# Block products for pair 2 of the first feed-forward part, and joined weight halves for the first dilated group's values

## The chip, the cores and the metric

One core of one Trainium2 chip runs the whole layer as one program. Its engines work side by side: TensorE (PE) multiplies, VectorE (DVE) and ScalarE (ACT) compute element by element, GpSimd (POOL) does a few small things, and SyncE (SP) issues nearly all transfers, one after another in program order. The metric is the device time of one execution in microseconds. The kernel before takes 1127.27 us (median of three runs, 1127.23 to 1127.75).

## What is computed

One decoder layer on 512 tokens of 1024 features in float32: a feed-forward half-step, a token mixer (sparse attention beside dilated attention, merged by gates), and a second feed-forward half-step. What matters here, cut from the reference:

```python
def swiglu(x, w_gate, w_up, w_down):
    return (jax.nn.silu(x @ w_gate) * (x @ w_up)) @ w_down
...
    h = rms_norm(x, ffn1_pre[l])
    x = x + 0.5 * rms_norm(swiglu(h, ffn1_w_gate[l], ffn1_w_up[l], ffn1_w_down[l]), ffn1_post[l])
    h = rms_norm(x, mix_pre[l])
    y = token_mixer(h, ...)
    x = x + rms_norm(y, mix_post[l])
    h = rms_norm(x, ffn2_pre[l])
    x = x + 0.5 * rms_norm(swiglu(h, ffn2_w_gate[l], ffn2_w_up[l], ffn2_w_down[l]), ffn2_post[l])
...
# dilated attention, for each of three (window, dilation) groups of four heads
    o, lse = banded_attention(strided(q), strided(k), strided(v), 1, window // dil, dil, slopes[gidx])
```

The feed-forward width is 2816, which is 22 blocks of 128.

## The kernel before

**Products in three parts.** To keep float32 precision every operand is split in a rounded high part and a low part: ScalarE casts the high part (`whi`, L112), VectorE subtracts it (`wlo`, L119). `mm3` (L141 to L143) then issues three matmuls: high by high, low by high, high by low. A `wsplit` of a 128x1024 piece is thus one ScalarE cast and one VectorE subtraction, and TensorE can't start a product before both parts stand.

**The feed-forward part** (`ffn`) goes through 11 pairs of feature blocks. A classical pair takes, for gate and up and both blocks, 8 steps of 128 input features with three matmuls of 512 tokens: 2 x 2 x 8 x 3 = 96 matmuls of 512 columns. The other pairs are done by `strassen(p)`: the pair's weights are four quarters (a11 and a12 are gate, a21 and a22 are up, each for one half of the 1024 input features), the tokens likewise, and Winograd's scheme makes gate and up with seven products in place of eight, on sums: 7 x 2 x 4 x 3 = 168 matmuls of 256 columns. The sums of the weights are made on VectorE, s1 = a21+a22 first, then a11-a21, s2 = s1-a11, and a12-s2. The sums of the tokens (`token_sums`, T1 to T4, in high and low parts) are made once, in steps taken from a list between the pairs. Before, pairs 3 to 10 of the first part are done in this way and pairs 0 to 2 classically.

**The down product** (`ffn_down`) is a scheme of seven products as well. It needs four sums of down weights for each pair (`down_sums`, T1 to T4, where T4 = b21 - T2). They are made ahead, while the pairs run (`weight_sums`, or `early_sums` from four separate blocks of 128x512), written to a tensor in memory (`tdram`), and loaded again when the products come. T4's product has 5 of its 11 weight blocks loaded into the tiles of the split tokens (`xl_t`, split there into `xh_t` and `xl_t`), which are free by then.

**Order.** Tiles come from pools, and a load waits until the last reader of its tile is done; the program's order on each engine is the order of the code. All loads and stores named here stand in one queue (SP): a transfer that waits holds all behind it. The gate and up weights of a Strassen pair are loaded at L361 in four pieces of 512 KB, the two quarters of the first half into one tile and those of the second half into another; of the second half the up quarter comes first.

**The dilated group 0's values** (from the line with `C_VD` on): for each of 4 groups of tokens, 8 steps of three matmuls of 256 columns; `keep` then stores a high part (ScalarE) and a low part (VectorE).

Of the kernel before, what the change touches and what calls it, by code (L numbers as in the profile page):

```python
# [63 lines left out]
class Layer:  # L64
# [237 lines left out]
    def ffn(self, n, wg, wu, wd, post, finish, xsrc, tags, nps, aside=None):  # L302
# [26 lines left out]
        def weight_sums(p):  # L329
# [6 lines left out]
            with self.tc.issue_after(self.last_rest):  # L336
                self.down_sums(*[r[:, e, h * S:(h + 1) * S] for e in range(2) for h in range(2)])
# [13 lines left out]
        def strassen(p):  # L351
# [45 lines left out]
            weight_sums(p)  # L397
# [81 lines left out]
        self.ffn_down(E, X, Y, wd, post, finish, xsrc)  # L479

    def down_sums(self, b11, b12, b21, b22):

        for out, x, y in ((b11, b12, b11), (b12, b22, b12), (b22, b22, b11), (b21, b21, b22)):
            self.nc.vector.tensor_sub(out, x, y)

    def early_sums(self, p, wd, places):
# [20 lines left out]
    def token_sums(self):  # L507
# [9 lines left out]
        self.tsum = [([], []) for _ in range(4)]
        steps = []
        for c in range(2):
            hi, lo = [[v.rearrange("p (k c) -> p k c", k=2) for v in g]  # L520
                      for g in (places[8 * c:8 * c + 4], places[8 * c + 4:8 * c + 8])]
            if kept:
                whole = [kept[h][i][c] for i, h in ((0, 0), (1, 1), (0, 1), (1, 0))]
            else:
                whole = [self.slot("x").rearrange("p (k c) -> p k c", k=2) for _ in range(4)]
            f1, f2, f3, f4 = whole
# [1095 lines left out]
```

## Time and profile before

| | us |
|---|---|
| runs | 1127.23, 1127.27, 1127.75 |
| profiled execution | 1127.8 |
| its span on the core | 1125.6 |
| TensorE busy | 1115.7 (99%) |
| VectorE busy | 911.2 (81%) |
| ScalarE busy | 646.8 (57%) |
| moved by DMA | 206 MB |

The span runs from the first to the last instruction in the trace; 2.2 us of the execution's own time lie around it. In the rows below, a group or timeline row names the line of the kernel, the engine, the operation, and out<-in by the program's tile names; `SPq` is the queue of SyncE, whose rows show when a transfer was issued, not when it landed. `pb_S`, `pb_T`, `pb_V` and `pb_F` are accumulators of TensorE. The profile's clock was 1.00 in all stretches shown.

### The profile page before, as it was taken

What the parts mean: (1) busy time and instruction counts of PE and PEld (TensorE: products, weight loads), DVE (VectorE), ACT (ScalarE), POOL (GpSimd) and SP (SyncE); (2) the same over time, 40 slices, a digit from 0 to 9 for tenths busy, and PEclk for the clock granted to TensorE, in tenths of its full rate; (3) what the DMA queues carried; (4) which work ended last, traced back from release to release, by engine and by line L of the source; (5) the groups of instructions that cost most, each with busy time, mean ns of one, the idle gap of its engine ahead of it and who ended that gap; (6) DMA issues with size and microseconds to landing.
All of it is one profiled execution on the core that took longest, in us unless ns stands there. A gap on an engine that the chain in (4) does not pass through costs nothing.

```text
span 1125.6 us, 18656 instructions
## 1 busy us (share of the span) xinstructions
PE 1115.7 (99%) x6998; PEld 1004.2 (89%) x6998; DVE 911.2 (81%) x1565; ACT 646.8 (57%) x1169; POOL 79.2 (7%) x112
## 2 busy tenths in 40 slices
PE   9999999999999999999999999999999999999997
PEld 8889999998889987778888998888999999998886
DVE  7889999879677889687666688976898888979674
ACT  5435555567564778677565634645555555558562
POOL 1000000000012033243000000001000000000000
PEclk9999999999999999999999999999999999999999
DMA  9986665578863652211477758683323434356862
GB/s 318 331 283 224 185 208 173 153 267 293 265 206 108 196 132 85 68 37 47 147 246 237 243 174 289 203 290 121 101 87 126 129 112 126 100 187 228 290 224 82
DMA packets 153086, 206.04 MB, mean 183 GB/s; under 512 B 19842, under 2 KB 98210, under 8 KB 152740
## 3 DMA queue, kind: packets, MB, share of 16 engines
q1 hardware_dynamic: 152992, 204.85, 56.2%
q8 instruction: 55, 0.90, 0.3%
q14 instruction: 35, 0.29, 0.1%
q10 hardware_dynamic: 4, 0.00, 0.0%
HBM read 165.45 MB, written 39.37 MB: 182 GB/s over the span
## 4 chain that ended last, share of the span: by engine, by line
PE 90%; DVE 5%; ACT 2%; issue 1%; POOL 1%; DMA 1%; POOLq 0%; DVEq 0%; ACTq 0%
PE pb_F L141 11%; PE pb_F L143 11%; PE pb_F L142 11%; PE pb_S L143 8%; PE pb_S L142 8%; PE pb_S L141 8%; PE pb_T L143 6%; PE pb_T L142 6%; PE pb_T L141 6%; PE pb_V L143 3%; PE pb_V L142 3%; PE pb_V L141 3%; PE pb_V L1060 2%; PE pb_T L1045 1%; DVE SP_s L785 1%
## 5 line engine op out<-in xcount | busy, mean ns | idle before, releaser
L112 ACT CAST whi<-raw 128x1024 fp32r<-128x1024 f32 (+1 forms) x213 | 217.7, 1023 | 245.6 <-issue 71.1
L119 DVE TENSOR_TENSOR wlo<-raw,whi 128x1024 fp32r<-128x1024 f32 (+1 forms) x213 | 252.9, 1190 | 91.8 <-ACT whi L112 89.9
L141 PE MATMUL pb_F<-xh_t,whi 128*128 128x512 f32 (+1 forms) x392 | 142.0, 362 | 0.2 <-DVE Q_s L1270 0.2
L142 PE MATMUL pb_F<-xl_t,whi 128*128 128x512 f32 (+1 forms) x392 | 141.1, 360 | 0.0
L143 PE MATMUL pb_F<-xh_t,wlo 128*128 128x512 f32 (+1 forms) x392 | 141.0, 360 | 0.0
L112 ACT CAST whi<-tmp_t 128x1024 fp32r<-128x1024 f32 x55 | 57.6, 1048 | 57.4 <-PE pb_S L142 22.4
L119 DVE TENSOR_TENSOR wlo<-tmp_t,whi 128x1024 fp32r<-128x1024 f32 x55 | 67.3, 1224 | 23.2 <-ACT whi L112 21.8
L141 PEld LDWEIGHTS pb_F<-xh_t,whi 128*128 128x128 f32 x392 | 74.2, 189 | 9.9 <-DVE Q_s L1270 0.4
L143 PEld LDWEIGHTS pb_F<-xh_t,wlo 128*128 128x128 f32 x392 | 74.2, 189 | 9.6
L142 PEld LDWEIGHTS pb_F<-xl_t,whi 128*128 128x128 f32 x392 | 74.3, 190 | 9.3
L141 PE MATMUL pb_S<-xh_t,whi 128*128 128x256 f32 (+1 forms) x232 | 68.4, 295 | 0.0
L143 PE MATMUL pb_S<-xh_t,wlo 128*128 128x256 f32 (+1 forms) x232 | 68.3, 294 | 0.0
L142 PE MATMUL pb_S<-xl_t,whi 128*128 128x256 f32 (+1 forms) x232 | 68.3, 294 | 0.0
L1036 POOL TENSOR_SCALAR SP_s<-SP_s,st_t 128x384 f32<-128x384 f32 (+2 forms) x48 | 47.8, 1010 | 103.8 <-DVE st_t L972 76.3
L163 POOL TENSOR_TENSOR rs_t<-rs_t,mhalf_t 128x1 f32<-128x1 f32 x24 | 17.1, 711 | 538.1 <-DVE rs_t L159 538.0
L142 PE MATMUL pb_T<-xl_t,whi 128*128 128x256 f32 (+1 forms) x184 | 53.9, 293 | 0.0
L143 PE MATMUL pb_T<-xh_t,wlo 128*128 128x256 f32 (+1 forms) x184 | 53.8, 293 | 0.0
L141 PE MATMUL pb_T<-xh_t,whi 128*128 128x256 f32 (+1 forms) x184 | 53.7, 293 | 0.0
L141 PEld LDWEIGHTS pb_S<-xh_t,whi 128*128 128x128 f32 x232 | 44.5, 192 | 1.0
L142 PEld LDWEIGHTS pb_S<-xl_t,whi 128*128 128x128 f32 x232 | 44.5, 192 | 1.0
L143 PEld LDWEIGHTS pb_S<-xh_t,wlo 128*128 128x128 f32 x232 | 44.5, 192 | 0.9
L785 DVE CUSTOM_DVE_ANT_0 SP_s<-pb_S,W_s 128x128 f32<-128x128 f32 (+2 forms) x92 | 37.9, 441 | 7.0 <-PE pb_S L780 4.8
(839 smaller groups left out, 3425.3 us busy)
## 6 DMA issues: line engine op xcount, KB each, us to landing
raw<-in_ffn_w_up_dram SPq DMA_DIRECT2D x38, 512.0 KB, 4.9
raw<-in_ffn_w_gate_dram SPq DMA_DIRECT2D x37, 512.0 KB, 5.0
raw<-in_w_in_dram SPq DMA_DIRECT2D x18, 1024.0 KB, 5.5
raw<-in_ffn_w_down_dram SPq DMA_DIRECT2D x14, 1024.0 KB, 5.8
raw<-tdram SPq DMA_DIRECT2D x14, 1024.0 KB, 6.5
NN_s<-in_ffn_w_down_dram SPq DMA_DIRECT2D x22, 512.0 KB, 5.0
tdram<-NN_s SPq DMA_DIRECT2D x22, 512.0 KB, 4.4
odram<-ring_s SPq DMA_DIRECT2D x36, 128.0 KB, 3.2
```

The source lines that it names most:

```text
L112: self.last_cast = self.nc.scalar.copy(dsthi, src).ins
L119: self.last_rest = self.nc.vector.tensor_sub(dstlo, src, dsthi.bitcast(F32)).ins
L141: mm(out, lhi, rhi, start=start, stop=False, skip_group_check=skip)
L142: mm(out, lhi, rlo, start=False, stop=False, skip_group_check=skip)
L143: mm(out, llo, rhi, start=False, stop=stop, skip_group_check=skip)
L163: nc.gpsimd.tensor_tensor(out=r, in0=v, in1=self.mhalf, op=OP.pow)
L785: nc.vector.tensor_tensor_reduce(p, s, w, -1.0, FLOOR, OP.add, OP.min, st_m)
L1036: nc.gpsimd.tensor_scalar(pp, pp, st[:, 1, t:t + 1], None, op0=OP.mult)
L1045: nc.tensor.transpose(b[:, o + (t - kk) * P:o + (t - kk + 1) * P], pt[pn][:, po + kk * P:po + (kk + 1) * P], self.ident)
L1060: self.nc.tensor.matmul(out[:, kk * P:S], v, pp, start=first and kk == 0 and pi == 0, stop=False, skip_group_check=True)
```

## The change

Five things are edited:

1. Pair 2 of the first part is done by `strassen` (`STRASSEN`).
2. For this, the token sums are made earlier. Two of the four transposed token groups are also copied unsplit while they are still in the accumulator (`whole=True` at the last two `norm_T`), so that four of the eight sums of high and low part (`join`) go; the list of steps (`STEPS`) now gives five steps at once, then three, then two.
3. T4 of five pairs (`DEFER`: 0, 1, 2, 9, 10) is not made ahead: `down_sums` leaves out its fourth subtraction, and the fourth place in memory holds b21 itself. At the end of the first part `ffn_down` loads T2 and b21 of these five pairs into `xl_t` and `xh_t` (four loads in place of one) and subtracts there. Those five are T4's first blocks in place of pairs 0 to 4.
4. A Strassen pair makes the down sums of the pair before it, not its own, and the tiles that `early_sums` uses for pairs 4 to 7 are others (`SUM_TAGS`).
5. The values of dilated group 0: the high and the low part of the weights stand side by side, so that the high part of the tokens meets both in one matmul of 512 columns, and the low part of the tokens meets the high part in one of 256. The right half of the accumulator is added to the low part of the values by one more VectorE instruction for each token group.

```diff
-STRASSEN = range(3, NF // 2), range(1, NF // 2)
+STRASSEN = range(2, NF // 2), range(1, NF // 2)
+DEFER = 0, 1, 2, 9, 10
-STEPS = (0, 3, 3, 3, 3), (4, 2)
+STEPS = (5, 3, 2), (4, 2)
...
-                self.down_sums(*[r[:, e, h * S:(h + 1) * S] for e in range(2) for h in range(2)])
+                self.down_sums(*[r[:, e, h * S:(h + 1) * S] for e in range(2) for h in range(2)], p not in DEFER)
...
-            weight_sums(p)
+            if p - 1 in STRASSEN[n]:
+                weight_sums(p - 1)
...
-        for out, x, y in ((b11, b12, b11), (b12, b22, b12), (b22, b22, b11), (b21, b21, b22)):
+        for out, x, y in ((b11, b12, b11), (b12, b22, b12), (b22, b22, b11), (b21, b21, b22))[:3 + last]:
             self.nc.vector.tensor_sub(out, x, y)
...
-        nc.sync.dma_start(xl[:, 0:EARLY].bitcast(F32), weights["T4"](0, EARLY))
+        if defer:
+            for k, o, m in ((0, 0, 3), (3, NP - 2, 2)):
+                for v, nm in ((xl, "T2"), (xh, "T4")):
+                    nc.sync.dma_start(v[:, k:k + m].bitcast(F32), weights[nm](o, m))
+        else:
+            nc.sync.dma_start(xl[:, 0:EARLY].bitcast(F32), weights["T4"](0, EARLY))
         product(half(parts["O"], 0), "B21", a, False, True, lambda k: split_next("Y"))
         for k in range(0, EARLY, 2):
             ks = slice(k, min(k + 2, EARLY))
-            self.split(xh[:, ks], xl[:, ks], xl[:, ks].bitcast(F32))
+            src = xl[:, ks].bitcast(F32)
+            if defer:
+                d4 = self.sbt("tmp", [P, 2, S], bufs=2)[:, 0:ks.stop - k]
+                with self.tc.issue_after(self.last_rest):
+                    nc.vector.tensor_sub(d4, xh[:, ks].bitcast(F32), src)
+                src = d4
+            self.split(xh[:, ks], xl[:, ks], src)
...
-        ws = [self.wsplit(r[:, 4 * u:4 * u + 4], [4, 256]) for u in range(2)]
+        ws = []
+        for u in range(2):
+            for i, w in enumerate(self.wpair([2, 512])):
+                k = 4 * u + 2 * i
+                v = w.rearrange("p k (x f) -> p k x f", x=2)
+                self.split(v[:, :, 0], v[:, :, 1], r[:, k:k + 2])
+                ws.extend((w[:, j], v[:, j, 0]) for j in range(2))
...
-            for k in range(KT):
-                w = ws[k // 4]
-                self.mm3(b[:, 0:256], self.xh[k][:, c], self.xl[k][:, c], w[0][:, k % 4], w[1][:, k % 4], k == 0, k == KT - 1)
-            vt[0].append(keep(b[:, 0:256], 0, t))
+            for k, (both, hi) in enumerate(ws):
+                nc.tensor.matmul(b, self.xh[k][:, c], both, start=k == 0, stop=False, skip_group_check=True)
+                nc.tensor.matmul(b[:, 0:256], self.xl[k][:, c], hi, start=False, stop=k == KT - 1, skip_group_check=True)
+            v = keep(b[:, 0:256], 0, t)
+            nc.vector.tensor_add(v[:, :, 1], b[:, 256:512].rearrange("p (n d) -> p n d", n=4), v[:, :, 1].bitcast(F32))
+            vt[0].append(v)
...
-            t2 = self.norm_T(2, g, OPEN[2], sq2)
+            t2 = self.norm_T(2, g, OPEN[2], sq2, whole=True)
```

How this moves instructions is seen at three places. The first is SyncE's queue ahead of the first Strassen pair's weights. Before (pair 3; `raw_874` is its first half of gate and up, `raw_877` the second half, `KB_s` are the blocks of down weights of `early_sums`, `tdram` the memory of the sums; in brackets what a row waits for):

```order
L494 DMA tdram_72<-KB_s_681 128x512 [waits DMAHW7_49,DVE_49]
L490 DMA KB_s_779<-in_ffn1_w_down_dram 128x512 [waits DMAHW4_49,DMAHW0_49]
L490 DMA KB_s_780<-in_ffn1_w_down_dram 128x512 [waits DMAHW5_49,DMAHW1_49]
L490 DMA KB_s_781<-in_ffn1_w_down_dram 128x512 [waits DMAHW6_49,DMAHW2_49]
L490 DMA KB_s_782<-in_ffn1_w_down_dram 128x512 [waits DMAHW7_49,DMAHW3_49]
L361 DMA raw_874<-in_ffn1_w_gate_dram 128x4x256
L361 DMA raw_874<-in_ffn1_w_up_dram 128x4x256
L475 DMA odram_73<-W_s_531 128x512 [waits DVE_49]
L494 DMA tdram_72<-KB_s_779 128x512 [waits DVE_49]
L494 DMA tdram_72<-KB_s_780 128x512 [waits DMAHW0_49,DVE_49]
L494 DMA tdram_72<-KB_s_782 128x512 [waits DMAHW1_49,DVE_49]
L361 DMA raw_877<-in_ffn1_w_up_dram 128x4x256 [waits DMAHW2_49,DVE_49,Activation_49]
```

And after (pair 2; `raw_715` and `raw_718` are its halves, `raw_622` the two blocks of down weights of pair 1):

```order
L492 DMA KB_s_691<-in_ffn1_w_down_dram 128x512 [waits DMAHW7_49,DMAHW3_49]
L492 DMA KB_s_692<-in_ffn1_w_down_dram 128x512 [waits DMAHW4_49]
L492 DMA KB_s_693<-in_ffn1_w_down_dram 128x512 [waits DMAHW5_49,DMAHW1_49]
L492 DMA x_s_1888<-in_ffn1_w_down_dram 128x512 [waits DMAHW2_49,Activation_49]
L496 DMA tdram_72<-KB_s_692 128x512 [waits DMAHW0_49]
L362 DMA raw_715<-in_ffn1_w_gate_dram 128x4x256 [waits DVE_49,Activation_49]
L362 DMA raw_715<-in_ffn1_w_up_dram 128x4x256
L339 DMA tdram_72<-raw_622 128x2048 [waits DMAHW6_49,DVE_49]
L496 DMA tdram_72<-KB_s_690 128x512 [waits DMAHW7_49,DVE_49]
L496 DMA tdram_72<-KB_s_691 128x512 [waits DVE_49]
L496 DMA tdram_72<-KB_s_693 128x512 [waits DMAHW1_49,DVE_49]
L362 DMA raw_718<-in_ffn1_w_up_dram 128x4x256 [waits DMAHW2_49,Activation_49]
```

The first half's loads now stand behind the store of a block (`KB_s_692`, b21 of pair 2) that nothing is subtracted from and that waits only for its own load, and between the two halves stand 1.8 MB of stores.

The second place is VectorE at the sums of that pair's weights. Before (the rows of L377, L379 and L383 are s1, a11-a21 and s2):

```order
L377 TENSOR_TENSOR tmp_t_880<-raw_874,raw_877 128x1024 [waits DMAHW5_49,DMAHW2_49]
L437 TENSOR_TENSOR ring_s_705<-ring_s_705,pb_T_744 128x512 [waits PE_49]
L119 TENSOR_TENSOR CB_s_480<-x_s_488,PT_s_476 128x512 [waits Activation_49]
L466 TENSOR_TENSOR SP_s_863<-ring_s_705 128x256 [waits DVE_49]
L119 TENSOR_TENSOR wlo_888<-raw_874,whi_887 128x1024 [waits DMAHW4_49,Activation_49]
L379 TENSOR_TENSOR raw_874<-raw_874 128x1024
L383 TENSOR_TENSOR tmp_t_881<-tmp_t_880,raw_874 128x1024
```

And after:

```order
L120 TENSOR_TENSOR wlo_729<-raw_715,whi_728 128x1024 [waits DMAHW4_49,Activation_49]
L378 TENSOR_TENSOR tmp_t_721<-raw_715,raw_718 128x1024 [waits DMAHW5_49,DMAHW2_49]
L380 TENSOR_TENSOR raw_715<-raw_715 128x1024 [waits DVE_49]
L384 TENSOR_TENSOR tmp_t_722<-tmp_t_721,raw_715 128x1024
L439 TENSOR_TENSOR W_s_550<-W_s_550,pb_S_661 128x512 [waits PE_49,Activation_49]
L120 TENSOR_TENSOR wlo_758<-raw_715,whi_757 128x1024 [waits Activation_49]
```

The subtraction and s2 follow s1 at once, and the low part of the first product's weights stands ahead of s1, not behind it.

The third place is SyncE's queue at the last products of the first part, where B21's weights and T4's first blocks are loaded. Before:

```order
L95 DMA raw_3415<-in_ffn1_w_down_dram 128x4x512 [waits DMAHW2_49,DVE_49]
L95 DMA raw_3465<-in_ffn1_w_down_dram 128x4x512 [waits DMAHW3_49,DVE_49]
L683 DMA xl_t_2887<-tdram_72 128x5x512 [waits DMAHW4_49,PE_49]
L95 DMA raw_3507<-in_ffn1_w_down_dram 128x3x512 [waits DMAHW6_49,DMAHW5_49,DVE_49]
L95 DMA raw_3557<-in_ffn1_w_down_dram 128x4x512 [waits DMAHW2_49,DVE_49]
```

And after:

```order
L96 DMA raw_3520<-in_ffn1_w_down_dram 128x4x512 [waits DMAHW5_49,DVE_49]
L670 DMA xl_t_2989<-tdram_72 128x3x512 [waits DMAHW6_49,PE_49]
L670 DMA xh_t_2988<-tdram_72 128x3x512 [waits DMAHW7_49]
L670 DMA xl_t_2989<-tdram_72 128x2x512 [waits DMAHW0_49,PE_49]
L670 DMA xh_t_2988<-tdram_72 128x2x512 [waits DMAHW1_49]
L96 DMA raw_3570<-in_ffn1_w_down_dram 128x4x512 [waits DMAHW2_49,DVE_49]
L96 DMA raw_3612<-in_ffn1_w_down_dram 128x3x512 [waits DMAHW3_49,DVE_49]
```

The second load of B21 (`raw_3465` before, `raw_3570` after) now stands behind the loads of T4's blocks, and these move twice the bytes.

More of the change, by code (lines that the diff above doesn't have):

```diff
@@ L478, in ffn, with down_sums @@
             E.append((hi, lo))
-        self.ffn_down(E, X, Y, wd, post, finish, xsrc)
-    def down_sums(self, b11, b12, b21, b22):
-        for out, x, y in ((b11, b12, b11), (b12, b22, b12), (b22, b22, b11), (b21, b21, b22)):
+        self.ffn_down(E, X, Y, wd, post, finish, xsrc, () if n else DEFER)
+    def down_sums(self, b11, b12, b21, b22, last=True):
+        for out, x, y in ((b11, b12, b11), (b12, b22, b12), (b22, b22, b11), (b21, b21, b22))[:3 + last]:
             self.nc.vector.tensor_sub(out, x, y)
@@ L491, in early_sums @@
         with self.tc.issue_after(self.last_rest):
-            self.down_sums(*places)
+            self.down_sums(*places, p not in DEFER)
         for (i, h), v in zip(blocks, places):
@@ L515, in token_sums @@
             places += [v[:, o:o + S] for o in range(0, v.shape[1], S)]
+        joined = 0 not in self.whole
+        if joined:
+            self.new_whole(0)
         kept, self.whole = self.whole, {}
@@ L521, in token_sums @@
                       for g in (places[8 * c:8 * c + 4], places[8 * c + 4:8 * c + 8])]
[L522 to L526, printed above, removed]
+            f1, f2, f3, f4 = whole = [kept[h][i][c] for i, h in ((0, 0), (1, 1), (0, 1), (1, 0))]
             for i in range(4):
@@ L605, in split_next, with product @@
             parts[nm].append((hi, lo))
-        def product(a, wname, banks, start, stop, side=None, tail=0, keep=None, between=None, pre=()):
+        def product(a, wname, banks, start, stop, side=None, tail=0, keep=None, between=None, pre=(), begin=0, end=NP):
             held = []
@@ L613, in mm @@
                 hi, lo = a(k, t)
-                self.mm3(banks[t], hi, lo, w[0], w[1], start and k == 0, stop and k == NP - 1, True)
-            for k, w in enumerate(pre):
+                self.mm3(banks[t], hi, lo, w[0], w[1], start and k == 0, stop and k == end - 1, True)
+            for k, w in pre:
                 for t in range(2):
                     mm(t, k, w)
-            for k0 in range(len(pre), NP, 4):
-                n = min(4, NP - k0)
+            for k0 in range(begin, end, 4):
+                n = min(4, end - k0)
                 r = self.raw(weights[wname](k0, n), [n, S])
@@ L623, in product @@
                     m = min(2, n - k1)
-                    if keep and k0 + k1 + m > NP - tail:
+                    if keep and k0 + k1 + m > end - tail:
                         for j in range(m):
@@ L632, in product @@
                         k = k0 + k1 + j
-                        if k >= NP - tail:
+                        if k >= end - tail:
                             held.append((k, (hi[:, j], lo[:, j])))
@@ L720, in ffn_down @@
         product(half(parts["O"], 256), "T4", c, False, True, None, NP - EARLY, list(HOLD_TAGS), between,
-                [(xh[:, k], xl[:, k]) for k in range(EARLY)])
+                [(k, (xh[:, i], xl[:, i])) for i, k in enumerate(defer or range(EARLY))],
+                *((3, NP - 2) if defer else (EARLY, NP)))
         r = self.rstd([self.meansq(c[1], S, 2.0), ms[3, 1]], 2.0)
```

38 lines of the change are left out of this document (12 added, 26 removed).

## The prediction

> **What bounds the kernel now.** I read the page first, then who waits for whom on TensorE, then five stretches around the edited pair. Busy time and instructions:
>
> ```profile
> span 1125.6 us, 18656 instructions
> PE 1115.7 (99%) x6998; PEld 1004.2 (89%) x6998; DVE 911.2 (81%) x1565; ACT 646.8 (57%) x1169; POOL 79.2 (7%) x112
> ```
>
> TensorE is busy for 1115.7 of 1125.6 us, so the kernel ends when its matmuls end; a change pays if it shortens their row, and costs if it opens a hole in it. The waits of TensorE, longest first:
>
> ```profile
> PE pb_V L1511 <- POOL ident_t masks.py:199: 1.5, 1, 1.5
> PE pb_S L779 <- DVE SP_s L988: 0.2, 1, 0.2
> ...
> PE pb_S L779 <- DVE st_t L785: 0.2, 1, 0.2
> ```
>
> After 1.5 us at the start no wait is over 0.2: the first part has no holes. The stretches (PE, weight load, DVE, ACT, POOL busy; clock; DMA share; GB/s) are the start, the time to the landing of the first Strassen pair's weights, and pairs 2, 3 and 4:
>
> ```profile
> 0.00:58.00 58.00, 56.55 (x338) 49.83 (x339) 46.73 (x76) 27.79 (x47) 7.23 (x16) 1.00 0.97 324
> 58.00:75.20 17.20, 17.20 (x78) 14.25 (x77) 12.18 (x20) 6.44 (x9) 0.00 (x0) 1.00 0.82 256
> 58.85:80.62 21.77, 21.77 (x98) 18.03 (x96) 16.74 (x25) 6.70 (x10) 0.00 (x0) 1.00 0.88 285
> 80.62:100.88 20.26, 20.26 (x170) 20.20 (x168) 20.05 (x24) 11.40 (x15) 0.00 (x0) 1.00 0.73 236
> 100.88:121.04 20.16, 20.16 (x171) 20.16 (x169) 20.04 (x27) 10.92 (x15) 0.00 (x0) 1.00 0.67 216
> ```
>
> Two things are to be seen. A classical pair (pair 2, its 96 matmuls) takes 21.77 us, a Strassen pair (168) 20.16. And to 58 us the DMA engines are 97% busy at 324 GB/s: at the start this kernel is short of transfers, and TensorE hides it only because every load was asked for early enough.
>
> **The change on TensorE.** The spacing of matmuls, in order of time (512 columns, then 256):
>
> ```profile
> 75.18 0.39 PE L141 MATMUL pb_V<-xh_t,whi 128*128 128x512 f32 x1
> 75.40 0.39 PE L142 MATMUL pb_V<-xl_t,whi 128*128 128x512 f32 x1
> ...
> 100.88 0.28 PE L141 MATMUL pb_T<-xh_t,whi 128*128 128x256 f32 x1
> 101.00 0.28 PE L142 MATMUL pb_T<-xl_t,whi 128*128 128x256 f32 x1
> ```
>
> One starts 0.12 us after another at 256 columns, and 21.77/96 = 0.2268 at 512 (the 0.39 and 0.28 overlap). Pair 2 as block products: 168 x 0.12 = 20.16 for 96 x 0.2268 = 21.77, **-1.61 us**. The values of group 0: of 96 products of 256 columns, 64 become 32 of 512, which is 32 x (3 x 0.12 - 0.2268 - 0.12) = 32 x 0.0132 = **-0.42 us**. Together -2.03, if nothing waits.
>
> [...]
>
> **VectorE's share.** Its rows before the first Strassen pair, and ScalarE's cast of that pair's second left operand:
>
> ```profile
> 75.22 1.23 DVE L377 TENSOR_TENSOR tmp_t<-raw 128x1024 f32<-128x1024 f32 x1 [2.16 <-DMA raw<-in_ffn_w_up_dram]
> 76.36 0.68 DVE L437 TENSOR_TENSOR ring_s<-ring_s,pb_T 128x512 f32<-128x512 f32 x1
> 76.95 0.69 DVE L119 TENSOR_TENSOR CB_s<-x_s,PT_s 128x512 fp32r<-128x512 f32 x1
> 77.56 0.42 DVE L466 TENSOR_TENSOR SP_s<-ring_s 128x256 f32<-128x256 f32 x1
> 77.89 1.22 DVE L119 TENSOR_TENSOR wlo<-raw,whi 128x1024 fp32r<-128x1024 f32 x1
> 79.03 1.22 DVE L379 TENSOR_TENSOR raw<-raw 128x1024 f32<-128x1024 f32 x1
> 80.16 1.22 DVE L383 TENSOR_TENSOR tmp_t<-tmp_t,raw 128x1024 f32<-128x1024 f32 x1
> ```
>
> ```profile
> 80.36 1.05 ACT L112 CAST whi<-raw 128x1024 fp32r<-128x1024 f32 x1 [6.30 <-DVE raw L379]
> ```
>
> A 128x1024 subtraction holds VectorE for 1.14 us, 128x512 for 0.60, 128x256 for 0.33. Pair 2 adds four sums and three splits of 128x1024 (7 x 1.14 = 8.0) and some 2 us of halves; four joins (2.4) and five fourth subtractions (3.0) go. That is about +4.6 us on an engine with 214 us free over the span. Its cover is thin in the Strassen pairs, 20.05 of 20.26: I cost the sum at nothing since five of the removed halves fall in this phase; if the cover were gone, the bound is 4.6 us, spread over nine pairs that have 0.1 to 0.2 of slack each. The moved token sums are the same rows earlier; the eight ScalarE copies of transposed tokens take 8 x 0.3 (a third of the 1.05 of a cast four times as large, with its start) on an engine with 28 of 58 us busy. The dilated values' four extra 256-element adds cost 4 x 0.33 on VectorE beside 2.8 us of matmuls each; at worst the last adds 0.3 to the end of its bank, at best nothing: I take 0.
>
> **The wait that it brings.** What pair 2 lacks is its weights. In the order shown above, the second product's left operand (a11-a21) stands on VectorE right behind s1 = a21+a22, and s1 needs the up weights of the second half (`raw_718`). In the row at 75.22 the same operand of pair 3 landed 5.4 us ahead of that pair's start (80.62); four other rows fitted between. Pair 2 starts at 58.86. Call the landing L. From it: s1 1.14, the subtraction and the cast 81.41 - 79.03 = 2.38, so the high part is there at L+3.5; VectorE goes on with s2 (1.14) and a sum of 128x512 (0.60), then the low part (1.23): L+5.2. The third matmul of product 2 needs that low part, and would come at 58.86 + 24 x 0.12 + 0.24 = 61.98. With 0.1 for the semaphores, as between 80.25 and 80.36, the hole is **S = L - 56.6**. Behind s1 on VectorE stand pair 1's last sums too; their bank comes free at L+4.0, ahead of product 3, so they add nothing.
>
> L must be put together from the queue:
>
> ```profile
> 29.66 0.35 SPq L338 DMA_DIRECT2D tdram<-raw  x1
> ...
> 38.23 0.38 SPq L95 DMA_DIRECT2D raw<-in_ffn_w_down_dram  x1
> ...
> 51.93 3.73 SPq L494 DMA_DIRECT2D tdram<-KB_s  x4
> 56.80 3.16 SPq L490 DMA_DIRECT2D KB_s<-in_ffn_w_down_dram  x4
> ...
> 69.00 0.38 SPq L361 DMA_DIRECT2D raw<-in_ffn_w_up_dram  x1
> ```
>
> ```profile
> 43.63 2.15 DVE L484 TENSOR_TENSOR raw<-raw 128x512 f32<-128x512 f32 x3 [0.63 <-DMA raw<-in_ffn_w_down_dram]
> ```
>
> ```profile
> tdram<-KB_s SPq DMA_DIRECT2D x12, 256.0 KB, 4.8
> KB_s<-in_ffn_w_down_dram SPq DMA_DIRECT2D x8, 256.0 KB, 5.4
> raw<-in_ffn_w_up_dram SPq DMA_DIRECT2D x3, 512.0 KB, 8.1
> ```
>
> (The last three: issues from 27 to 77 us, KB each, median us to landing.) Adding up tile sizes, the queue through `raw_718`'s up weights holds 18.74 MB after; before, it held 22.41 for pair 3's, and 18.74 through the four stores issued from 51.93. Three ways to L:
> - Bytes alone: 58 us x 324 GB/s = 18.8 MB, so L = 57.9 and S = 1.3.
> - Before's own queue: the four loads at 56.80 wait each for one of those stores, and leave one by one to about 59.6; by then 18.74 MB had landed. L = 59.6, S = 3.0.
> - The chain of the new order: the 1 MB store of down sums (row 29.66; 11.9 MB through it, 11.7 after) held the load behind it until 38.23; that load landed at 43.63; the first store behind it lands 0.26 MB/324 = 0.8 later, 44.4, and only then may the KB load of pair 2's down weights leave; the second of these leaves 0.5 later and lands at 50.3 (5.4). Now comes what is new: its block is not subtracted from, so its store is next in the queue, waits for that landing, and holds all gate and up loads of pair 2 behind it. From there 3.67 MB to the end of the wanted load: at 324 GB/s 11.3 us, L = 61.6; at the 256 of the second stretch 14.3, L = 64.6.
>
> I take 61.6, since only this way counts the waits in the queue, and the DMA engines stay full behind such a wait as they were to 58: S = 5.0. The ends for the range are 0 and 8.0. The wait is not made good later: TensorE has no idle time to give back.
>
> **The end of the first part.** T4 of five pairs is now made from two loads each:
>
> ```profile
> 288.28 4.32 SPq L95 DMA_DIRECT2D raw<-in_ffn_w_down_dram  x2
> 293.90 0.37 SPq L683 DMA_DIRECT2D xl_t<-tdram  x1
> 296.64 11.76 SPq L95 DMA_DIRECT2D raw<-in_ffn_w_down_dram  x3
> ```
>
> 2.6 MB for 1.3, and ahead of B21's second load, not behind it. At 256 to 324 GB/s 1.3 MB more is 4 to 5 us, against loads that were issued 4 us apart and were not waited for. I take 0; the other bound is 5.1 - 4 = 1.1 us late. Three more subtractions (2 x 1.14 + 0.60) and the same three splits stand there beside 15 us of B21's matmuls. Stores of T4's five blocks stay; only their content differs.
>
> **The sum.** -1.61 - 0.42 + 5.0 = +3.0. The profiled execution took 1127.8 us (1125.6 and 2.2 around it), 0.5 over the median of the runs, 1127.27, so I add to the median: **1130.2 us**. A measurement of this kernel can tell about 0.2% (2.25 us) from no change, so it reads as slower once S exceeds 4.3, that is L over 60.9.
>
> **Rivals.**
> 1. *The weights are in time*: S = 0 if L is 56.6 or less, 1125.2 us (-0.18%, not slower). For it: 3.67 MB less stand ahead than for pair 3. Against it: that needs 331 GB/s from the first microsecond, over the 324 at 97% share, with no wait in the queue. Chance 0.13, of which 0.05 falls below 1125.0. [...]
> 2. *A short wait*: L from 57 to 60.9, as the first two ways give: 1125.5 to 1129.5, read as the same. Chance 0.22.
> 3. *A long one*: the slower rate (S = 8.0, 1133.2), or B21's load late as well (1.1): to 1134.3. For it the 256 GB/s of the second stretch. Chance 0.06.
> 4. *Spacing in proportion to columns*: 0.2268/2 = 0.1134 at 256. The pair then saves 21.77 - 168 x 0.1134 = 2.7, the values nothing: 1124.6 without a hole, faster. The rows at 100.88 and 101.00 speak against it. Chance 0.03. [...]
> 5. *VectorE becomes the bound* in pairs 3 to 10, up to 4.6 us more: it leaves 0.1 to 0.2 a pair. It ends where the forecast does and I count it there.
>
> The forecast, a hole of 4.3 to 8 us (1129.5 to 1133.2), keeps 0.56. Slower is 0.56 + 0.06, the same 0.22 + 0.08, faster 0.05 + 0.03. The range from 1125.2 (no hole) to 1133.6 (just past the slower rate) leaves out 0.08 below and about 0.05 above; the forecast's own is 1129.5 to 1133.2.
>
> **What would show it.** In the waits of TensorE: a new first row, a bank of `NN_s,whi` waiting for ScalarE's cast of `raw` and VectorE's `wlo`, 4 to 8 us together; on VectorE an idle stretch before the first `tmp_t<-raw` of L378 ended by the DMA of the up weights at 60 to 64. Pair 2 without that hole 20.2 us. At the dilated values, 32 matmuls of 512 columns and 32 of 256 in 11.1 us for 11.5. In the queue, the store that follows the KB loads held until near 50 us. The prediction is wrong if that load lands by 58, if the new order of the queue brings the gate and up loads forward more than I read, or if a later pair waits too: then the hole is elsewhere.

## The result: slower by 1.2%, and the profile after

The changed kernel takes 1139.99 us (median of four runs, 1139.61 to 1145.7) against 1127.51 of the kernel before: a ratio of 1.0119, interval [1.0104, 1.0133]. I had forecast 1130.2, in a range to 1133.6. The direction and the main mechanism, a hole in pair 2 behind a held queue, were right; its size was not. One name on record is wrong: `KB_s_692`, which the part on the change calls b21 of pair 2 (and the prediction a block of pair 2's down weights), is a block of pair 9, whose sums are made ahead here. That nothing is subtracted from it, and that its store comes early, is as described.

The page of the kernel after, its span and busy times:

```profile
span 1138.4 us, 18785 instructions
...
PE 1117.6 (98%) x7038; PEld 1005.2 (88%) x7038; DVE 918.1 (81%) x1575; ACT 654.6 (58%) x1187; POOL 76.0 (7%) x112
```

TensorE's busy time rose by 1.9 us, the span by 12.8: the loss is idle time. The waits of TensorE (line, what it waited for, us in total, times, longest):

```profile
PE pb_V L142 <- ACT whi L113: 7.1, 1, 7.1
...
PE pb_V L144 <- DVE wlo L120: 0.9, 1, 0.9
PE pb_S L144 <- DVE wlo L120: 0.9, 1, 0.9
```

The first row is the forecast hole, a bank of pair 2 (L142, `pb_V`) that waits for ScalarE's cast, and the second belongs to it; the last is in pair 1. Where the time went is read from when the same matmul starts in the two traces. The kernel after is late by 1.3 us where pair 2 begins, by 11.2 where pair 3 begins, by 10.9 at 305 us of the kernel before, by 13.1 at 349, by 13.3 behind the dilated values and by 12.9 at the end. So pair 2 costs 9.9 us, pair 1 before it 1.3, and the end of the first part 2.2; nothing else is lost. Pair 1's part is this execution's: the profiles of experiments 3 to 8 and 10, which defer as well, lose 0.1 us at most between 30 us and pair 2.

VectorE around the hole (start, us, what; in brackets the idle time ahead and what ended it), then TensorE:

```profile
67.10 1.23 DVE L378 TENSOR_TENSOR tmp_t<-raw 128x1024 f32<-128x1024 f32 x1 [6.35 <-DMA raw<-in_ffn_w_up_dram]
...
70.64 0.68 DVE L439 TENSOR_TENSOR W_s<-W_s,pb_S 128x512 f32<-128x512 f32 x1
71.23 1.22 DVE L120 TENSOR_TENSOR wlo<-raw,whi 128x1024 fp32r<-128x1024 f32 x1
```

```profile
63.42 0.28 PE L144 MATMUL pb_T<-xh_t,wlo 128*128 128x256 f32 x1
70.77 0.58 PE L142 MATMUL pb_V<-NN_s,whi 128*128 128x256 f32 x1 [7.07 <-ACT whi L113]
71.15 0.42 PE L143 MATMUL pb_V<-N_s,whi 128*128 128x256 f32 x1
72.50 0.58 PE L144 MATMUL pb_V<-NN_s,wlo 128*128 128x256 f32 x1 [0.94 <-DVE wlo L120]
72.88 0.41 PE L142 MATMUL pb_V<-NN_s,whi 128*128 128x256 f32 x1
73.10 0.41 PE L143 MATMUL pb_V<-N_s,whi 128*128 128x256 f32 x1
...
77.67 0.28 PE L144 MATMUL pb_S<-NN_s,wlo 128*128 128x256 f32 x1
```

The up quarter landed at L = 67.1, not 61.6. From it the chain runs as worked out: high part at 70.7 (L+3.6 for L+3.5), low part at 72.5. The product starts on the high part alone (70.77), and its third matmul (72.50) is the first to wait for the low part: both need not stand first, as the section on the kernel before has it. Start to start, the two holes are 63.42 to 70.77 and 71.15 to 72.50, less 0.12 each: 8.5 us. After them matmuls come 0.21 us apart until 77.36, where they came 0.12 apart ahead of the holes (63.30 to 63.42). Two stretches say why (us, then busy times of PE, PEld, DVE, ACT and POOL, the granted clock, DMA share, GB/s):

```profile
67.25:77.49 10.24, 5.79 (x25) 5.49 (x26) 10.21 (x13) 4.19 (x6) 0.00 (x0) 0.50 0.85 273
78.00:80.00 2.00, 2.00 (x19) 2.00 (x18) 2.00 (x4) 1.50 (x3) 0.00 (x0) 1.00 1.05 393
```

The granted clock fell to 0.50 during the hole, at 67.25, and came back at 77.49: from 70.77 to 77.67 the matmuls took 2.6 us more than at 0.12. The prediction had no term for a clock of 0.50 in and behind a hole of 7.1 us. In experiment 8 the clock fell behind one hole of 1.8 us (last section).

The queue of SyncE explains L (start, us of issue, transfer):

```profile
15.38 0.92 SPq L492 DMA_DIRECT2D of_s<-in_ffn_w_down_dram  x2
22.56 0.33 SPq L496 DMA_DIRECT2D tdram<-KB_s  x1
...
52.39 0.33 SPq L496 DMA_DIRECT2D tdram<-KB_s  x1
...
56.83 0.77 SPq L362 DMA_DIRECT2D raw<-in_ffn_w_up_dram  x1
```

Before, loads go on at that place (`V_s` from 15.11, `of_s` at 20.11, gate weights at 20.82); here a store of `KB_s` stands behind the two loads into `of_s` and is issued at 22.56. Its block is not subtracted from, so it comes early in the program's order, and waits for its own load while all loads behind it wait too. It happens again at 52.39. The first 58 us as one stretch, and two parts of it, of the kernel after:

```profile
0.00:58.00 58.00, 54.80 (x332) 47.43 (x333) 43.01 (x71) 28.18 (x54) 5.93 (x16) 1.00 0.87 279
22.00:26.00 4.00, 4.00 (x37) 4.00 (x36) 2.79 (x6) 3.06 (x9) 0.00 (x0) 1.00 0.52 148
38.00:42.00 4.00, 4.00 (x20) 3.29 (x19) 4.00 (x7) 0.78 (x2) 0.00 (x0) 1.00 0.15 60
```

and the two parts of the kernel before, where the whole stretch had 0.97 and 324 GB/s:

```profile
22.00:26.00 4.00, 4.00 (x36) 4.00 (x35) 3.56 (x7) 1.08 (x2) 0.00 (x0) 1.00 1.07 373
38.00:42.00 4.00, 4.00 (x19) 3.33 (x18) 4.00 (x10) 1.35 (x4) 0.60 (x1) 1.00 0.69 209
```

In 22 to 26 us the DMA engines are half idle, in 38 to 42 nearly wholly; the second is the hold that the prediction knew, a load behind the 1 MB store of down sums, and it ends at 41.06 where it ended at 38.23 before. Over 58 us that is 45 GB/s less, 2.6 MB that are still to come, 8 us at 324 GB/s.

### The profile page after: what moved, and what is told of

Same layout as the page of the kernel before. It is cut to its first block, busy times and chain, and to the rows that moved or that the text cites. A ratio compares the mean times of both kernels' runs of the same rounds, so it can differ in the third digit from the quotient of the medians.

```text
span 1138.4 us, 18785 instructions
## 1 busy us (share of the span) xinstructions
PE 1117.6 (98%) x7038; PEld 1005.2 (88%) x7038; DVE 918.1 (81%) x1575; ACT 654.6 (58%) x1187; POOL 76.0 (7%) x112
## 4 chain that ended last, share of the span: by engine, by line
PE 82%; DVE 8%; DMA 4%; ACT 3%; issue 2%; POOL 1%; SPq 0%; DVEq 0%; POOLq 0%; ACTq 0%
PE pb_F L142 10%; PE pb_F L144 10%; PE pb_F L143 10%; PE pb_S L144 7%; PE pb_S L143 7%; PE pb_S L142 7%; PE pb_T L144 5%; PE pb_T L143 5%; PE pb_T L142 5%; PE pb_V L144 2%; PE pb_V L143 2%; PE pb_V L142 2%; PE pb_V L1056 2%; PE pb_T L1041 1%; DMA raw<-in_ffn_w_gate_dram 1%
## 5 line engine op out<-in xcount | busy, mean ns | idle before, releaser
L120 DVE TENSOR_TENSOR wlo<-raw,whi 128x1024 fp32r<-128x1024 f32 (+1 forms) x211 | 249.7, 1187 | 90.3 <-ACT whi L113 88.6
L142 PE MATMUL pb_F<-xh_t,whi 128*128 128x512 f32 (+1 forms) x392 | 141.8, 362 | 0.1
L113 ACT CAST whi<-tmp_t 128x1024 fp32r<-128x1024 f32 x58 | 60.8, 1048 | 61.7 <-PE pb_S L143 23.4
L120 DVE TENSOR_TENSOR wlo<-tmp_t,whi 128x1024 fp32r<-128x1024 f32 x58 | 70.9, 1222 | 23.2 <-ACT whi L113 21.9
L142 PEld LDWEIGHTS pb_F<-xh_t,whi 128*128 128x128 f32 x392 | 74.2, 189 | 9.9 <-ACT x_s L234 0.3
L142 PE MATMUL pb_S<-xh_t,whi 128*128 128x256 f32 (+1 forms) x232 | 67.5, 291 | 0.0
L144 PE MATMUL pb_T<-xh_t,wlo 128*128 128x256 f32 x184 | 52.1, 284 | 0.3 <-DVE wlo L120 0.3
L142 PE MATMUL pb_T<-xh_t,whi 128*128 128x256 f32 x184 | 52.0, 283 | 0.3 <-DVE xl_t L225 0.3
L143 PE MATMUL pb_T<-xl_t,whi 128*128 128x256 f32 x184 | 52.1, 284 | 0.0
L142 PEld LDWEIGHTS pb_S<-xh_t,whi 128*128 128x128 f32 x232 | 44.5, 192 | 0.6
L120 DVE TENSOR_TENSOR PT_s<-pb_T,PT_s 128x512 fp32r<-128x512 f32 (+1 forms) x72 | 39.3, 560 | 5.6 <-ACT PT_s L113 4.7
```

The costliest lines, as they stand in the source:

```text
L113: self.last_cast = self.nc.scalar.copy(dsthi, src).ins
L120: self.last_rest = self.nc.vector.tensor_sub(dstlo, src, dsthi.bitcast(F32)).ins
L142: mm(out, lhi, rhi, start=start, stop=False, skip_group_check=skip)
L143: mm(out, lhi, rlo, start=False, stop=False, skip_group_check=skip)
L144: mm(out, llo, rhi, start=False, stop=stop, skip_group_check=skip)
```

## The experiments

Offsets below are differences in the start of the same matmul to the kernel before, in one profiled execution each; L is the start of pair 2's s1. "Deferral" is the part of the change by which T4 of five pairs is not made ahead.

**1. The values alone.** The kernel before with the edit of the dilated values, and nothing else.

> The kernel before with the dilated values' part alone. If the 512-column products save what the spacing of matmuls says, the values' stretch takes 11.1 us for 11.5 and the kernel 0.4 us less, 1127.1 for 1127.5. If the one more VectorE addition or the bank with both halves in use holds TensorE up, the gain is gone: 1127.5 or more.

Measured: 1129.39 us against 1128.33, ratio 1.0009 [0.9999, 1.0018], span 1127.7. From the start of their first matmul to the start of their last, the products of group 0's values take 11.39 us (631.62 to 643.01) where they took 11.44 (630.95 to 642.39): -0.05, forecast -0.42. And the matmul behind them waits longer than it did. Rows of VectorE, then of TensorE there, then TensorE's of before:

```profile
642.59 0.18 DVE L1240 TENSOR_TENSOR mn_t<-mn_t,nat_t 128x16 f32<-128x16 f32 x1 [3.77 <-DMA nat_t<-sdram]
...
643.56 0.42 DVE L1289 TENSOR_TENSOR Q_s<-pb_F,Q_s 128x256 fp32r<-128x256 f32 x1
```

```profile
643.01 0.28 PE L1287 MATMUL pb_F<-wlo,xl_t 128*128 128x256 f32 x1
644.13 0.47 PE L141 MATMUL pb_F<-xh_t,whi 128*128 128x512 f32 x1 [0.83 <-DVE z_t L1250]
```

```profile
642.39 0.28 PE L143 MATMUL pb_F<-whi,xl_t 128*128 128x256 f32 x1
642.85 0.51 PE L141 MATMUL pb_F<-xh_t,whi 128*128 128x512 f32 x1 [0.17 <-DVE Q_s L1270]
```

VectorE stands at the merge of the three groups' statistics (`mn_t`), which waits for a load, with the values' keep and the new addition (L1289) behind it. That load ends where it did (641.90 before; this execution is 0.7 us late as a whole), and TensorE waits 0.83 us where it waited 0.17: up to that matmul the stretch takes 12.51 us for 11.90.

**2. Without deferral.**

```diff
-DEFER = 0, 1, 2, 9, 10
+DEFER = ()
```

> The changed kernel with no pair deferred: all four sums of down weights are made ahead again, and the last products load T4 once. Theory A (the store of the unsubtracted block is ready first, stands early in the queue, and holds the loads behind it, at 22.6 and at 52.4 us): the up weights of pair 2 land at 60 to 62 instead of 67.1, TensorE's hole is 4 to 5 us for 8.4, and the 2.1 us lost in the last products come back: about 1131. Theory B (the bytes ahead of these weights set their landing, whatever the order): they land at 65 or later, and only the last products gain: 1137.

Measured: 1128.66 us against 1128.33, ratio 1.0005 [0.9995, 1.0016], span 1125.0. The first sum of pair 2 on VectorE, the queue, and TensorE in pair 2:

```profile
55.19 1.23 DVE L378 TENSOR_TENSOR tmp_t<-raw 128x1024 f32<-128x1024 f32 x1
```

```profile
47.58 1.63 SPq L362 DMA_DIRECT2D raw<-in_ffn_w_up_dram  x2
...
52.45 4.92 SPq L496 DMA_DIRECT2D tdram<-KB_s  x4
```

```profile
59.54:79.69 20.15, 20.15 (x169) 20.15 (x168) 19.60 (x24) 11.81 (x16) 0.00 (x0) 1.00 0.96 324
```

With all subtractions made ahead, no store is ready early, and the program's order puts the two up quarters into the queue together at 47.6, ahead of the stores; L is 55.2 or earlier (there is no wait ahead of it). From its first matmul to pair 3's, pair 2 takes 20.15 us without a hole (168 matmuls), on a VectorE that is busy for 19.60: the saving on pair 2 is real, and VectorE does not become the bound. The 2.2 us at the end of the first part are gone as well. Deferral is the cause of the loss.

**3. The early store moved back.** For a deferred pair the store of the unsubtracted block goes behind the other three.

```diff
+        order = list(zip(blocks, places))
+        if p in DEFER:
+            order.append(order.pop(2))
...
```

> The changed kernel, deferral kept, but the unsubtracted block's store is issued behind the other three stores of its pair. Theory A: the transfers don't pause at 22 to 26 us, the queue isn't held at 50 to 52, the up weights land at 62 to 63: about 1134. Theory B: 67, and 1140 as before it.

Measured: 1136.0 us, ratio 1.007 [1.0048, 1.0091], span 1132.1; 4.5 us late at pair 3. L is 60.85. Waits and clock:

```profile
PE pb_V L142 <- ACT whi L113: 1.6, 1, 1.6
PE pb_V L144 <- DVE wlo L120: 1.6, 1, 1.6
```

```profile
63.05:66.46 3.41, 0.50 (x2) 0.30 (x2) 3.41 (x6) 2.33 (x3) 0.00 (x0) 1.00 0.94 311
66.46:69.88 3.42, 3.29 (x15) 3.29 (x16) 3.42 (x6) 1.74 (x3) 0.00 (x0) 0.50 0.75 248
```

The order of two stores (pairs 10 and 9, both made ahead) brings 6 us of L. Behind two holes of 1.6 us with two matmuls between them the clock fell to 0.50 here, from 66.46 to 69.88.

**4. The hole filled.** Forty-eight matmuls of 256 columns that nobody reads, between the first and second product of pair 2.

```diff
+WARM = 48
...
             product(r11, w, b11, True, False)
+            if (n, p) == (0, 2):
+                for i in range(WARM):
+                    with self.tc.issue_after(self.last_mm):
+                        self.last_mm = nc.tensor.matmul(r7[:, 0:H], self.xh[i % 8][:, 0:P], self.xh[i % 8][:, 0:H],
...
```

> The changed kernel with 48 matmuls of 256 columns put into TensorE's hole, between products 1 and 2 of pair 2; their result is overwritten. If the granted clock of 0.5 at 67 to 77 us comes from TensorE's idle 7 us, the filled 5.8 us keep it at 1.0, the 24 matmuls behind take 0.12 each instead of 0.21, and the kernel takes 2.2 us less: 1137.8. If they are slow for another reason (operands, transfers), nothing changes: 1140.

Measured: 1138.08 us, ratio 1.0088 [1.0068, 1.0108], span 1137.0. L is 65.3, so the weights are as late as ever. Clock and spacing:

```profile
72.00:74.00 2.00, 2.00 (x19) 2.00 (x18) 2.00 (x5) 0.62 (x1) 0.00 (x0) 1.00 0.98 301
```

```profile
71.06 0.28 PE L144 MATMUL pb_V<-N_s,whi 128*128 128x256 f32 x1
71.17 0.28 PE L145 MATMUL pb_V<-NN_s,wlo 128*128 128x256 f32 x1
```

With the 48 matmuls in the hole the clock stays at 1.00, also behind the last holes (0.9 and 1.2 us), and matmuls are 0.12 apart where they were 0.21. So the half clock comes from the hole. What it costs on balance is less than the 2.6 us of the spacing: product 3 now reaches its weights too early and waits 1.1 us for ScalarE. Pair 3 starts 8.6 us late, 2.6 less than after, 1.8 of which the earlier landing may have given: 0.8 is left for the clock.

**5. The difference first.** In pair 2 a11-a21 is made ahead of s1, and s2 and s1 from it (s2 = a22-(a11-a21), s1 = s2+a11), so that product 2 does not need the late half. Same queue.

```diff
-            nc.vector.tensor_add(s1, a21, a22)
+            first_half = (n, p) == (0, 2)
+            if not first_half:
+                nc.vector.tensor_add(s1, a21, a22)
...
-            nc.vector.tensor_sub(s2, s1, a11)
+            if first_half:
+                nc.vector.tensor_sub(s2, a22, a21)
+                nc.vector.tensor_add(s1, s2, a11)
+            else:
+                nc.vector.tensor_sub(s2, s1, a11)
```

> The changed kernel with the same queue, but in pair 2 VectorE makes a11-a21 first, then s2 as a22-(a11-a21), then s1 as s2+a11. If the late up quarter is what TensorE waits for, product 2 runs without a wait, the hole moves to product 3, 2.9 us further on, and with s2 one subtraction nearer to the landing it is 4 to 5 us for 8.7; some half clock may stay: 1134 to 1136. If VectorE's own backlog (token sums made earlier) were the cause, the order of these three would change less than 1 us: 1139 to 1140.

Measured: 1137.86 us, ratio 1.0091 [1.0061, 1.012], span 1137.2, 7.0 us late at pair 3. The second product runs; the hole stands at the third:

```profile
PE pb_S L142 <- ACT pb_S L392: 6.4, 1, 6.4
```

The late half's first sum (s2 here) starts at 65.7. Of the 4.2 us gained at pair 3 the earlier landing may have given 1.4; the hole has moved on, and the clock falls here too (0.50 from 68.0 to 74.8 us).

**6. T4's loads behind B21's second load**, at the end of the first part.

```diff
+                    with self.tc.issue_after(self.last_raw):
+                        nc.sync.dma_start(v[:, k:k + m].bitcast(F32), weights[nm](o, m))
...
+        product(half(parts["O"], 0), "B21", a, False, True, lambda k: split_next("Y"), after=blocks4 if defer else None)
```

> The changed kernel with the loads of T4's five blocks queued behind B21's second load, as before, still twice the bytes. If the 2.1 us lost between 305 and 349 us come from B21's load standing behind them, the loss goes: 1138 in all, and 0 to 0.5 us lost there. If they come from the bytes themselves or from the three added subtractions, the loss stays or moves: 1140.

Measured: 1140.03 us, ratio 1.011 [1.0081, 1.0139]; still 2.2 us lost from 305 to 349. B21's load behind the blocks of T4, on which the prediction had its bound of 1.1, is not the reason there. Nor does VectorE wait for the blocks themselves: none of its three rows of L680 has idle time ahead of it. What is left is VectorE; the kernel after in order of time, then a row of before:

```profile
322.74 1.22 DVE L680 TENSOR_TENSOR tmp_t<-xh_t,xl_t 128x1024 f32<-128x1024 f32 x1
...
326.22 1.22 DVE L680 TENSOR_TENSOR tmp_t<-xh_t,xl_t 128x1024 f32<-128x1024 f32 x1
...
330.76 0.68 DVE L680 TENSOR_TENSOR tmp_t<-xh_t,xl_t 128x512 f32<-128x512 f32 x1
331.36 1.28 DVE L688 TENSOR_TENSOR pb_F<-pb_F,CP_s 128x512 f32<-128x512 f32 x2
```

```profile
318.14 0.69 DVE L693 TENSOR_TENSOR pb_F<-pb_F,CP_s 128x512 f32<-128x512 f32 x1
```

The three subtractions of L680 and their splits stand ahead of the scaling of the first part's output (L688; L693 before). With the 10.9 us of then it would have come at 329.0; it comes 2.3 later, and the next part's norm (`tmp_t`, L213) after it. TensorE's wait for that, the main part of 1.5 us lost there; the other 0.7 goes in small steps from 305 to 332 us of before:

```profile
356.39 1.32 PE L218 MATMUL pb_F<-ident_t,tmp_t 128*128 128x128 f32 x8 [1.01 <-DVE tmp_t L213]
```

**7. Pair 2 classical, the rest of the change kept.**

```diff
-STRASSEN = range(2, NF // 2), range(1, NF // 2)
+STRASSEN = range(3, NF // 2), range(1, NF // 2)
```

> The changed kernel with pair 2 done classically again; deferral, earlier token sums, places and the values' part stay. If the held queue is the cause by itself, pair 2's up weights still land near 67, where the classical pair wants them at 65 with cast and subtraction: a hole of 3 to 5 us, 1.3 us before pair 2 and 2.1 in the last products, 1133 to 1135. If it is the early need of the block products, only the last products lose: 1129.5.

Measured: 1139.12 us, ratio 1.0102 [1.0073, 1.0131], span 1137.0; 7.3 us lost in pair 2 though it is classical, in waits of 1.8, 1.7, 0.5 and 0.5 and matmuls at a clock of 0.50 from 70.5 to 73.9, and 1.2 at the end of the first part. It is not the block products that make the weights late.

**8. Fewer bytes ahead.** The down weights of later pairs are queued behind the gate and up weights of pair 2; deferral is kept.

```diff
+            if p in STRASSEN[0] and p not in AHEAD.values():
+                with self.tc.issue_after(self.pair2_load):
+                    self.nc.sync.dma_start(v, src)
...
```

> The changed kernel, deferral kept, but the loads of down weights for later pairs (2.1 MB of them stood ahead of pair 2's weights) are queued behind pair 2's. If bytes ahead set the landing, the up weights land 5 to 6 us sooner, at 61 to 62, and the kernel takes about 1132. If the holds set it (a store that waits at the head of the queue while the DMA engines idle), they land at 65 or later: 1137 to 1140.

Measured: 1137.59 us, ratio 1.0095 [1.007, 1.0119], span 1133.2; L is 59.5. Pair 2 is left with holes of 1.4 and 1.2 us, at a clock of 1.00, and pair 3 starts 1.5 us late. Its profile loses 3.5 us elsewhere, near 690 us: a wait of 1.8 (the one of experiment 11) and matmuls at a clock of 0.50 from 691.25 to 694.67 behind it. The bytes asked for ahead count beside the order.

**9. The merge late.** Without deferral, and the merge of the statistics on VectorE behind the third group of values.

```diff
+            if t == 2:
+                with self.tc.issue_after(low.ins):
+                    merge()
...
```

> No deferral (all four down sums made ahead, as in the kernel without DEFER), and the merge of the three groups' statistics issued on VectorE behind the third token group's kept values instead of ahead of the first. Theory (the joined values gain 0.5 us on TensorE, and lose it again because the first keep stands on VectorE behind the merge, which waits for the statistics' load): the bank after the values no longer waits, the offset at the values' end goes from -0.5 to -1.0 against the kernel without deferral, and the span is about 1124.5 (1125.0 there, 1125.6 before). Rival (that wait is the store of the values' or the banks' turn, not the merge): the wait of 0.5 to 1.1 stays, span 1125.0. Over all runs a difference to before of -0.5 to -1.5 us, ratio 0.9990, within 0.2%.

Measured: 1129.49 us against 1128.14, ratio 1.0009 [0.9999, 1.0019], span 1125.7. The wait behind the values is gone and the stretch gains 0.40 us (11.50 for 11.90), but not by the products: with the values as before and no wait behind them (experiment 12) it takes 11.57. The runs show nothing of the gain.

**10. Deferral of pairs 0 to 2 alone.** Pairs 9 and 10 have their fourth subtraction ahead again.

```diff
-            self.down_sums(*places, p not in DEFER)
+            self.down_sums(*places, p not in DEFER[:3])
...
-            if defer:
+            if defer and k < 3:
```

> Deferral kept for pairs 0 to 2 alone; pairs 9 and 10, made by early_sums, get their fourth subtraction ahead again, so that no store in the queue's start stands ready first. At the end T2 and b21 of three pairs are loaded and subtracted (two subtractions of 1024 and 512, for three). Theory (the store of an unsubtracted early block holds the queue): the up quarter lands near 59 to 61 as with the store moved back, the hole in pair 2 is under 3.5 us, the offset at pair 3's start 1 to 5 us for 11.2; the 2.2 us lost at the end of the first part stay at 1.2 to 2.2, since two of three subtractions stay: span 1128 to 1132. Rival A (the bytes hold it, not the order): 11 us at pair 3, span 1138. Rival B (the loss at the end comes from the T4 loads of pairs 9 and 10 alone): 0 at the end, span 1126 to 1130.

Measured: 1138.37 us, ratio 1.0093 [1.0074, 1.0112], span 1134.1; 6.6 us late at pair 3 and 0.9 more at the end of the first part. VectorE's first sum of pair 2, and TensorE's waits:

```profile
62.27 1.22 DVE L378 TENSOR_TENSOR tmp_t<-raw 128x1024 f32<-128x1024 f32 x1 [6.20 <-DMA raw<-in_ffn_w_up_dram]
```

```profile
PE pb_V L142 <- ACT whi L113: 3.9, 1, 3.9
...
PE pb_V L144 <- DVE wlo L120: 1.3, 1, 1.3
```

The unsubtracted early block accounts for 4.6 of the 12.1 us between the kernel after and the one without deferral at pair 3. In the rest the up quarter stands behind five stores and leaves at 56.5, for 47.6 there; the hole of 5.2 and the clock behind it (0.50 from 66.0 to 72.8 us) make it more than the 1 to 5 us expected. Rival A is out: the bytes are the same. At the end of the first part the loss is 0 with none of the subtractions and 0.9 with two; with three it is 1.2 to 2.2 in seven profiles (after, experiments 3 to 8). Rival B would have made it 0 here. That VectorE's order is the cause there is what the rows suggest; it wasn't isolated, and the scatter with three says that something else has a share.

**11. Nothing waits.** Experiment 9 with the edits of 5 and 8.

> The late merge without deferral, and in pair 2 also a11-a21 ahead of s1 and the down weights of later pairs loaded behind pair 2's. Theory (without deferral nothing waits in pair 2 any more): no gain over the late merge alone, span within 0.4 us of it (1124 to 1125). Rival (pair 1 and pair 2 still lose some 0.7 us to late loads there): 0.7 us less, 1123.8. Against before by all runs -0.5 to -2 us, which five rounds can just tell from nothing.

Measured: 1129.12 us, ratio 1.0006 [0.9996, 1.0016], span 1127.2. It is 1.35 us ahead of before at pair 3, and loses 2.6 near 684. VectorE and TensorE there:

```profile
684.07 0.69 DVE L494 TENSOR_TENSOR NN_s<-NN_s 128x512 f32<-128x512 f32 x1 [5.42 <-DMA NN_s<-in_ffn_w_down_dram]
...
685.82 0.68 DVE L120 TENSOR_TENSOR PT_s<-pb_T,PT_s 128x512 fp32r<-128x512 f32 x1
```

```profile
686.56 0.65 PE L1334 MATMUL pb_T<-ident_t,SP_s 128*128 128x128 f32 x4 [2.23 <-DVE PT_s L120]
```

A subtraction of down weights for the last part waits for its load until 684.07 (before, until 682.30), and the low part that TensorE needs stands behind it on VectorE. Of the twelve profiles with joined values six lose 0.8 to 3.5 us here, of the two without (before and experiment 12) none; two are too few to lay it to the joined values.

**12. Pair 2 alone.** No deferral, and the values as before.

> Pair 2 by block products and all down sums made ahead (no deferral), with the dilated values as before the change. Theory (the saving of pair 2 is real, and what blurs the runs of the kernels with joined values is a wait of 1 to 3.5 us near 684 us, where VectorE stands at a subtraction of down weights still on their way while TensorE comes 0.5 to 1 us earlier): the offset at pair 3 is -0.9 and stays; span 1124.7 to 1125.2; no such wait; the runs lie close together and the median of all is 0.7 to 1.0 us under before, ratio 0.9992. Rival A (that wait comes with any kernel that reaches that place earlier): the runs scatter from 1126 to 1131 as with joined values, median 1128 to 1129.5. Rival B (the saving of pair 2 does not last to the end): no scatter, and the median within 0.3 us of before.

Measured: 1126.41 us (1125.46 to 1129.35, 11 runs) against 1128.25, ratio 0.9986 [0.9977, 0.9995]: 1.8 us less, where 0.7 to 1.0 was expected. This is the one version that beats the kernel before, by 0.14%, less than the 0.2% that I called measurable but with an interval below 1. Beside experiment 2 (1.0005 [0.9995, 1.0016]) it suggests that the joined values cost more than they save (the two intervals just touch), and experiment 1 leans the same way. Pair 2 itself goes from 0.8 late to 0.3 early. The theory wanted the scatter gone, and it is not: the profiled execution is one of the longer ones (1127.79, span 1126.0), without the wait near 684 but with 0.9 at another place. Rivals A and B fall by the median (the trace can't test A: this execution comes to 684 us 0.6 late, not early); whether joined values bring the later wait more often, and why, stays open.

## Why the prediction was wrong, step by step

- **Pair 2, -1.61.** Right: 20.15 us without holes (experiment 2), for 21.77.
- **The values, -0.42: both steps failed.** With no wait behind them the joined products take 11.50 us and the separate ones 11.57 (experiments 9 and 12): -0.07. The sum had 32 pairs of matmuls at 0.347 us, 11.10; in experiment 1 they take 0.4 more, 0.25 of it at the first two matmuls of the third token group, right behind VectorE's new addition for the first group, whose bank it takes. And "their adds take 0" failed a second time: the next bank waits for VectorE, 0.83 us in experiment 1 for 0.17 before, and by the runs the edit costs 1 to 2 us (1.1 in experiment 1, whose interval just takes in none; 2.2 between experiments 2 and 12).
- **S = L - 56.6.** The relation held. With L at 67.1 and pair 2 starting 1.3 late it gives 9.2; the holes were 8.5, with 0.26 more at half clock between them. The rest is a small wait that pair 2's first product had already (0.4 at 60.80, for a low part): it shortens the hole. The sum of 128x512 stood ahead of the low part as forecast.
- **L = 61.6: the step that failed.** I counted the waits of the queue from 38 us on and took the earlier part over from before ("11.9 MB through it, 11.7 after"). But the unsubtracted block holds the queue from 16 to 22.6 us already. The second hold I had found, and put at 50.3; it came at 52.39. From there to the landing 3.67 MB took 14.7 us, not 11.3, though the engines were busy (0.97 and 319 GB/s): in that time 4.7 MB went, so 1.0 MB of other transfers had their share. Of the 5.5 us by which L was off, the later hold makes 2.1 and these transfers 3.4. Experiments 3 and 8 show both at work: the two stores moved back bring 6.2 us of L, fewer bytes ahead 7.6. The "slower rate", L = 64.6, was nearer for this reason.
- **The clock was not in the sum**: 2.6 us more. The forecast hole of 5 us would probably have had it too, as the smaller ones of experiment 3 did (two of 1.6 us, and 0.50 behind them). The trace of before has no hole in its first part in which to see it; its clock is at 0.50 only behind the last matmul (1121.8 to 1125.0 us).
- **Before pair 2** I had counted nothing; pair 1 waits once for its weights' low part, 0.9 in the list of waits, in this one execution of those that defer.
- **The end of the first part, 0 with a bound of 1.1**: 2.2 us (1.2 to 2.2 in other profiles). I looked at the loads and let "three more subtractions stand beside 15 us of matmuls" count as cover. They are covered as work, but they delay what stands behind them on VectorE.
- **VectorE as the bound** (rival 5): refuted, pairs 3 to 10 keep their length. Spacing in proportion (rival 4): refuted, 0.12. Rival 3, a long wait, was the nearest and its price too low; rival 1, weights in time, is what happens without deferral.

In sum: +1.3 before pair 2; -1.6 + 8.5 + 2.6 in it, and some 0.4 of small waits; +2.2 at the end; -0.6 elsewhere: 12.8, as measured.

## What to carry to other kernels

Work that is put off changes the order of the queue as well: a store whose data is ready as soon as it is loaded moves to the front of an in-order queue and holds every load behind it (here until 22.56 and 52.39 us), so cost a removed operation by the transfers that now come earlier. When a hole is forecast on TensorE, add the time at half clock behind it (2.6 us here behind 7.1; none behind 1.4 and 1.2 in experiment 8), and when instructions are added to a covered engine, look at what stands behind them, not only at the engine's free time. Compare a stretch between the same two marks in both traces: one that ends at the next start counts a wait as work. A gain that ends at an engine waiting for a load is no gain, and only the runs of each part by itself show which parts pay.

## What was not expected of the hardware

Behind two holes of 1.6 us, with two matmuls between them, the clock fell (experiment 3), while behind holes of 1.4 and 1.2 us it stayed at 1.00 (experiment 8). It was at 0.50 for 10.24 us after, for 3.42 in experiment 3, and for 6.8 in experiments 5 and 10. The holes can be laid beside each other in stretches of 3.41 us, about the shortest of these times. In experiment 3 both fall in the one that ends where the clock changes (63.05 to 66.46, TensorE busy for 15% of it), and the next is at 0.50. In experiment 8 they fall in two, the first rows here; a later hole of that execution, at 688 us, lies in one, which ends where the clock changes as well:

```profile
59.79:63.20 3.41, 2.05 (x19) 1.85 (x17) 3.38 (x4) 1.05 (x1) 0.00 (x0) 1.00 1.07 358
63.20:66.61 3.41, 2.17 (x16) 1.97 (x17) 3.41 (x6) 2.48 (x3) 0.00 (x0) 1.00 0.53 172
...
687.84:691.25 3.41, 1.57 (x11) 1.05 (x10) 3.28 (x5) 0.10 (x1) 0.00 (x0) 1.00 0.72 243
691.25:694.67 3.42, 3.42 (x15) 3.23 (x14) 3.28 (x9) 1.80 (x5) 0.00 (x0) 0.50 0.72 243
```

Busy for 60 and 64%, TensorE still has 1.00 behind them (to 80 us); at 688 us a single wait of 1.8 us leaves 46%, and 0.50 follows. These are rows of two profiled executions, found afterwards: how busy TensorE must be to keep its clock was not measured, and no run moved a hole to test it.
